# First MLP product of a two-layer trunk: weights stationary replaced by activations stationary, with a TensorE transpose of the squared ReLU

## The chip, the cores and the metric

The kernel runs on one core of one Trainium2 chip. The metric is the device time of one execution in microseconds (us), the median of three runs. Traces come from the hardware profiler: one profiled execution, with the busy time of each engine: PE (TensorE matmul), PEld (TensorE weight load), DVE (VectorE), ACT (ScalarE), POOL (GpSimd) and the SP queue that issues the weight transfers.

## What is computed

A trunk of two layers over 256 tokens of width 2048. Each layer has an attention and SSD part (not touched) and an MLP of width 8192 with squared ReLU:

```python
h = rmsnorm(x, ln2_g)
x = x + jnp.square(jax.nn.relu(h @ w_mlp_in)) @ w_mlp_out
```

All is float32. The norm's scale per token is kept out of `h` and applied (squared) where the second product is added to `x`, which squared ReLU allows.

## The kernel before

Every large product is made of float32r matmuls in three terms: each operand is split into a rounded part `hi` and a remainder `lo`, and the result is hi·hi + hi·lo + lo·hi, summed in PSUM.

The program is a list of **steps**. A step takes half of a weight panel (1024 elements on each of 128 partitions). Panels come by DMA into `raw` (three buffers), 1 MB each. `convert` makes the parts of a half panel: ACT casts `raw` to `hi` (line 121) and DVE subtracts to get `lo` (line 126). The emission loop (line 982) converts four steps ahead (`LA = 4`, five buffers of `hi` and of `lo`), then emits the step's matmuls, then its `post` if it ends an output group, then `tick`, which runs small tasks that are due. ACT, DVE and PE each work their own queue in the order of emission. `stages(f, g)` runs f in the tick right behind the step, and g one step later.

There are two kinds of product:

- `w_units`, **weights stationary**: for each block of 128 weight columns and each k tile of 128 rows, one matmul with 512 moving columns (the activations' whole and low part side by side: `hi` of the weights times both, line 215) and one with 256 (`lo` of the weights times the whole part, line 216; lines 218 and 219 for the last k). A step has 16 matmuls. The result stands transposed, hidden columns on the partitions, and `joined` adds its two halves (lines 425 and 426).
- `x_group`, **activations stationary**: for each k tile and each half of the tokens three matmuls with 512 moving weight columns (lines 291 to 293). A step has 12 matmuls: six for tokens 0 to 127, then six for tokens 128 to 255. The tokens are on the partitions.

Both kinds move 6144 columns per step. The MLP is worked in eight groups of 1024 hidden columns (`GF`). `mlp1(G)` makes `acts[G]`, the squared ReLU, split into hi and lo with the hidden columns on the partitions; `mlp2(G)` uses it as stationary operand. The order is `mlp1(0)`, then for each G `mlp1(G+1)`, `mlp2(G)`. Both have 16 steps a group. Before, `mlp1` is four `w_units` of 256 columns, and `mlp1_post` has for every 128 hidden columns: a copy of half of PSUM by ACT, DVE's sum, DVE's squared ReLU (line 822), and the split by ACT and DVE, on tiles of 128x256. PSUM holds four `acc` buffers, two `sa` and two `sb`.

Of the kernel before, what the change touches and what calls it, by code (L numbers as in the profile page):

```python
# [12 lines left out]
AF = mybir.ActivationFunctionType  # L13
# [18 lines left out]

# Columns of the shape-only constants.
K_ID, K_TRI, K_DIST, K_LNC, K_SEL, K_END = 0, 128, 256, 640, 1024, 1040
# Columns of the packed parameters, channels on the partitions.
V_G1, V_G2, V_GA, V_GS, V_DS, V_CW, V_CB, V_AL, V_DB, V_END = 0, 32, 64, 80, 96, 112, 208, 232, 264, 296
# [17 lines left out]
class Step:  # L54
    """Half a weight panel: its split into two float32r parts, and the products it goes into."""

# [11 lines left out]
def trunk_kernel(ctx: ExitStack, tc, x_in, xT_in, w_in, w_v, w_dt, w_out, w1, w2, final_g, par_in, cst_in, out):  # L68
# [27 lines left out]
    def k1(s="t1", w=T):  # L96
        return k1p.tile([P, w], F32, tag="k1", name=nm(s))
# [19 lines left out]
    def split(*parts):  # L117
        """hi + lo = src * g, each part of twelve significant bits."""
        for hi, lo, src, g in parts:
            if g is None:  # L120
                nc.scalar.copy(hi, src)  # L121
            else:
                nc.scalar.activation(hi, src, AF.Copy, scale=g)
        for hi, lo, src, g in parts:
            if g is None:
                nc.vector.tensor_tensor(lo, src, hi.bitcast(F32), op=ALU.subtract)  # L126
            else:
                nc.vector.scalar_tensor_tensor(lo, src, g, hi.bitcast(F32), op0=ALU.mult, op1=ALU.subtract)  # L128

    mm = nc.tensor.matmul  # L130

# [1 line left out]
    cst = const.tile([P, K_END], F32, name="cst")  # L133
# [51 lines left out]

# [1 line left out]
    tasks = []  # L187
# [14 lines left out]
    def stages(*fs, delay=1):  # L202
        """The first after this step or a later one, each other one a step later."""
        def g():
            for f in fs:
                f()
                yield 1
        spawn(g(), delay)

    steps = []  # L210

# [1 line left out]
    def whole_and_low(ps, wh, wl, r, k):  # L213
# [7 lines left out]
    def w_units(units, hT):  # L221
        """Weights stationary: out[col, token | its low part's products]. Two units at a time share
        the order of k so that the later half of the activations may come late."""
        def unit_steps(u):
            st = {}
            panels = [Panel(u["src"](kh), [P, 8, T]) for kh in range(2)]

            def mk(kq):
                def f(hi, lo):
                    if kq == 0:  # L230
                        st["ps"] = [acc(), acc()]
                    hv = hi.rearrange("p (k c) -> p k c", k=4)
                    lv = lo.rearrange("p (k c) -> p k c", k=4)
                    h = hT()
                    for ti in range(2):
                        ps = st["ps"][ti]
                        cs = slice(ti * P, (ti + 1) * P)
                        for kk in range(4):
                            k = kq * 4 + kk
                            r = h[k // 8][:, k % 8, :]  # L240
                            whole_and_low(ps, hv[:, kk, cs], lv[:, kk, cs], r, k)
                return f

            def post():
                for ti in range(2):
                    u["post"](ti, st["ps"][ti])

            return [Step(panels[kq // 2], kq % 2, mk(kq), post if kq == 3 else None) for kq in range(4)]

        for a in range(0, len(units), 2):  # L250
            ss = [unit_steps(u) for u in units[a:a + 2]]
            if a == 0 and len(ss) == 2:
                steps.extend(ss[0][:2] + ss[1][:2] + ss[0][2:] + ss[1][2:])
            else:
                for s in ss:
                    steps.extend(s)

    def x_group(src, nk, h_of, post, apart=False):
        """Activations stationary: out[token, 512 columns] over nk tiles of k. Apart: all of the first
        128 tokens before the second, and post by their halves."""  # L260
        st = {}
# [38 lines left out]
    def wide(w, l, r0, c0):  # L300
        """The panel of 512 rows and 512 columns from r0, c0."""
        return w[l, r0 // 512, c0 // 512]

    def tall(w, l, r0, c0):
        """The panel of 1024 rows and 256 columns from r0, c0."""
        return w[l, r0 // 1024, c0 // T]

# [1 line left out]
    def new_h():  # L309
# [5 lines left out]
    class Norm:  # L315
        """Sums of squares and split transposes of x, by its chunks of 512 columns."""

# [38 lines left out]
    def channel_rstd(ssq, n):  # L356
        """From squares with the channels on the partitions."""
        ps = sa()
        for t in range(2):
            mm(ps[:, t:t + 1], ssq[:, t * P:(t + 1) * P], ones[:, 0:1], start=True, stop=True)  # L360
        return finish_rstd(ps[:, 0:2], n)

    class FirstNorm:
        """The same from the transposed input, by its chunks of 512 channels."""

# [35 lines left out]

# [1 line left out]
    def layer(l, S, S_next):  # L403
        """S: this layer's state, with hT and norm of its first sub-layer; S_next: the next one's."""
        def rstdB_task():
# [14 lines left out]
        def joined(ps, n=P, scale=None):  # L420
            """The two halves of a weights-stationary product, summed."""
            p2 = p2p.tile([P, T], F32, tag="p2", name=nm("p2"))
            u = k1("u")
            if scale is None:
                nc.scalar.copy(p2[:n], ps[:n, T:2 * T])  # L425
                nc.vector.tensor_tensor(u[:n], ps[:n, 0:T], p2[:n], op=ALU.add)  # L426
            else:
                nc.scalar.mul(p2[:n], ps[:n, T:2 * T], scale)
                nc.vector.scalar_tensor_tensor(u[:n], ps[:n, 0:T], scale, p2[:n], op0=ALU.mult, op1=ALU.add)
            return u  # L430

        # x, B and C: convolution and SiLU, channels on the partitions.
        xs_t, bc_t = {}, {}
# [61 lines left out]

        # dt, the weights' two parts side by side: out[part and head, token | its low part's products].
        dts = {}
# [15 lines left out]
        steps.append(Step(Panel(w_dt[l], [P, 16, 16]), 0, dt_mm, dt_post))  # L513
        # v, tokens on the partitions.
        vt = {}
# [11 lines left out]

# [1 line left out]
        ssd = {}  # L529

        def ssd_prep():
            # dt = softplus(raw + bias), tokens on the partitions.
            ps = sa()
# [34 lines left out]
            yield 2  # L568
            # Running sums of dt * a in each chunk, and the decay to the first chunk's end.
            ps = sa()  # L570
# [48 lines left out]
        def ssd_group(g):  # L619
            """The group's inputs times dt, and its state after the first chunk."""  # L620
            xs, dt, dtd = xs_t["xs"], ssd["dt"], ssd["dtd"]
# [21 lines left out]
        def ssd_pair(j):  # L643
# [3 lines left out]
            for i in range(2):  # L647
                mm(ps[:, i * T:(i + 1) * T], sel[:, 2 * j + i:2 * j + i + 1].to_broadcast([32, P]), cumT,
                   start=True, stop=True)
            # Decays from s to t: where s is later than t, the exponent's bound keeps them finite and  # L650
            # cbs is zero.
            MT = ep.tile([P, 2, T], F32, tag="MT", name=nm("MT"))
# [47 lines left out]

# [1 line left out]
        att = {}  # L702
# [19 lines left out]
        def att_head(j, i):  # L722
            """Softmax of one head's scores; transposed, it is left in att["pt", h]."""
            q, k = att["qk", j, 0], att["qk", j, 1]
# [57 lines left out]

# [1 line left out]
        def out_post(c, which, ps):  # L784
# [28 lines left out]

# [1 line left out]
        acts = {}  # L815

        def mlp1_post(G, f, ps):
            if f == 0:
                acts[G] = new_m()
            u = joined(ps)  # L820
            a = k1("a")
            nc.vector.scalar_tensor_tensor(a, u, 0.0, u, op0=ALU.max, op1=ALU.mult)  # L822
            m = acts[G][:, f, :]
            split((m[:, 0:T], m[:, T:2 * T], a, None))

        def mlp1(G):
            w_units([dict(src=lambda kh, u=u: tall(w1, l, kh * 1024, G * GF + u * T),
                          post=lambda ti, ps, u=u: mlp1_post(G, 2 * u + ti, ps)) for u in range(4)],
                    lambda: S["hT2"])

# [37 lines left out]
    class Final:  # L868
        """The last norm and the output."""

# [46 lines left out]

# [1 line left out]
    panels = []  # L919
# [124 lines left out]
```

## Time and profile before

| | |
|---|---|
| median of 3 runs | 2235.57 us (2235.47 to 2235.91) |
| span of the profiled execution, first to last instruction | 2233.3 us |
| the median less that span | 2.3 us |
| PE busy | 2208.7 us (99%) |
| PEld, DVE, ACT busy | 1850.0, 1460.3, 1058.4 us |
| mean granted TensorE clock | 0.998 of full |

The profiled execution is known by its span; what lies around the span is taken from the timed runs. Matmuls overlap in the records (a matmul's own duration is longer than the distance to the next), so what a matmul costs is read from the distance between starts.

### The profile page before, as it was taken

To read this page: it belongs to the slowest core of one execution; us is meant where nothing else is said; L and a number is where in the kernel's file an instruction comes from. 1 tells how busy PE (TensorE), PEld (TensorE's weight loads), DVE (VectorE), ACT (ScalarE), POOL (GpSimd) and SP (SyncE) were. 2 spreads that over 40 slices of the span, in tenths; PEclk is the share of its full clock that TensorE was granted. 3 is DMA by queue.
4 is the path that set the end of the run, shared out by engine and by line. 5 is a ranking of instruction groups with operands and counts; after the bars stand their busy time and mean duration, and the time that the engine had idled before them with its cause. 6 is when DMAs were issued, how large, how long until landed. Compare 5 with 4: busy or idle time off the path is not lost.

```text
span 2233.3 us, 29120 instructions
## 1 busy us (share of the span) xinstructions
PE 2208.7 (99%) x11444; PEld 1850.0 (83%) x11444; DVE 1460.3 (65%) x1997; ACT 1058.4 (47%) x1539; POOL 150.6 (7%) x201
## 2 busy tenths in 40 slices
PE   8999999999999999999999999999999999999998
PEld 6877778888888888888888777788888888888886
DVE  7757986665665655656666578866656656656565
ACT  6544554543444444434555455555444434444443
POOL 3102310000000000000011032100000000000001
PEclk9999999999999999999999999999999999999999
DMA  8454344555555555555554543455555555555554
GB/s 295 172 188 145 121 151 170 188 188 190 189 189 189 189 188 192 186 196 190 180 188 168 174 150 124 145 186 184 185 190 195 189 189 189 188 191 187 188 193 147
DMA packets 58249, 404.44 MB, mean 181 GB/s; under 512 B 6400, under 2 KB 6784, under 8 KB 10240
## 3 DMA queue, kind: packets, MB, share of 16 engines
q1 hardware_dynamic: 58112, 402.58, 52.1%
q8 instruction: 90, 1.47, 0.3%
q14 instruction: 47, 0.39, 0.0%
HBM read 400.45 MB, written 2.10 MB: 180 GB/s over the span
## 4 chain that ended last, share of the span: by engine, by line
PE 95%; DVE 3%; issue 1%; ACT 0%; DMA 0%; POOL 0%; SPq 0%; ACTq 0%; POOLq 0%; DVEq 0%
PE acc L215 30%; PE acc L216 15%; PE acc L291 14%; PE acc L293 14%; PE acc L292 14%; PE acc L219 2%; PE acc L218 1%; DVE lo L126 1%; PE sb L729 1%; PE sb L728 1%; DMA raw<-in_w_in 0%; PE sb L748 0%; PE sb L765 0%; PE acc L505 0%; DVE h L128 0%
## 5 line engine op out<-in xcount | busy, mean ns | idle before, releaser
L126 DVE TENSOR_TENSOR lo<-raw,hi 128x1024 fp32r<-128x1024 f32 x752 | 921.5, 1235 | 613.4 <-ACT hi L121 613.1
L121 ACT CAST hi<-raw 128x1024 fp32r<-128x1024 f32 x754 | 783.3, 1048 | 718.6 <-PE acc L293 414.2
L215 PE MATMUL acc<-h,hi 128*128 128x512 f32 x3000 | 1077.0, 401 | 8.7 <-DVE h L128 8.7
L216 PE MATMUL acc<-h,lo 128*128 128x256 f32 x3000 | 843.4, 281 | 2.2 <-DVE lo L126 2.2
L215 PEld LDWEIGHTS acc<-h,hi 128*128 128x128 f32 x3000 | 565.3, 188 | 147.1 <-issue 10.2
L216 PEld LDWEIGHTS acc<-h,lo 128*128 128x128 f32 x3000 | 568.3, 189 | 11.4 <-DVE lo L126 2.5
L291 PE MATMUL acc<-hi,m 128*128 128x512 f32 x1280 | 501.0, 391 | 0.0
L293 PE MATMUL acc<-hi,m 128*128 128x512 f32 x1280 | 498.3, 389 | 0.0
L292 PE MATMUL acc<-lo,m 128*128 128x512 f32 x1280 | 498.1, 389 | 0.0
L291 PEld LDWEIGHTS acc<-hi,m 128*128 128x128 f32 x1280 | 240.3, 188 | 51.5 <-issue 3.0
L293 PEld LDWEIGHTS acc<-hi,m 128*128 128x128 f32 x1280 | 240.3, 188 | 50.2
L292 PEld LDWEIGHTS acc<-lo,m 128*128 128x128 f32 x1280 | 240.4, 188 | 49.2
L121 ACT CAST m<-a 128x256 fp32r<-128x256 f32 x128 | 52.1, 407 | 153.6 <-DVE a L822 153.6
L425 ACT COPY p<-acc 128x256 f32<-128x256 f32 x186 | 68.9, 370 | 66.6 <-PE acc L219 61.4
L126 DVE TENSOR_TENSOR m<-a,m 128x256 fp32r<-128x256 f32 x128 | 54.4, 425 | 60.5 <-ACT m L121 60.5
L833 DVE SCALAR_TENSOR_TENSOR x_sb<-acc,r,x_sb 128x512 f32<-128x512 f32 x128 | 89.9, 743 | 4.9 <-PE acc L293 4.9
L426 DVE TENSOR_TENSOR u<-acc,p 128x256 f32<-128x256 f32 x186 | 77.2, 417 | 17.1 <-ACT p L425 17.0
L219 PE MATMUL acc<-h,hi 128*128 128x512 f32 x200 | 80.0, 400 | 0.0
L353 POOL TENSOR_TENSOR rstd<-ms,nhalf 128x2 f32<-128x2 f32 x10 | 8.8, 882 | 873.9 <-DVE ms L351 862.7
L822 DVE SCALAR_TENSOR_TENSOR a<-u 128x256 f32<-128x256 f32 x128 | 54.4, 425 | 4.4
L218 PE MATMUL acc<-h,lo 128*128 128x256 f32 x200 | 56.6, 283 | 0.0
L886 POOL TENSOR_TENSOR x_sb<-x_sb,final_g 128x512 f32<-128x512 f32 x6 | 8.6, 1454 | 687.3 <-DMA final_g<-in_final_norm_g 672.1
(167 smaller groups left out, 1169.7 us busy)
## 6 DMA issues: line engine op xcount, KB each, us to landing
raw<-in_w_mlp_in SPq DMA_DIRECT2D x128, 1024.0 KB, 4.9
raw<-in_w_mlp_out SPq DMA_DIRECT2D x128, 1024.0 KB, 4.9
raw<-in_w_in SPq DMA_DIRECT2D x69, 1024.0 KB, 4.9
raw<-in_w_out SPq DMA_DIRECT2D x32, 1024.0 KB, 4.8
raw<-in_w_v SPq DMA_DIRECT2D x16, 1024.0 KB, 4.9
raw<-in_w_in SPq DMA_DIRECT2D x6, 512.0 KB, 9.0
xT<-in_xT SPq DMA_DIRECT2D x4, 512.0 KB, 8.6
x_sb<-in_x SPq DMA_DIRECT2D x4, 512.0 KB, 6.5
```

Source lines behind the costliest of these rows:

```text
L121: nc.scalar.copy(hi, src)
L126: nc.vector.tensor_tensor(lo, src, hi.bitcast(F32), op=ALU.subtract)
L215: mm(ps, wh, r, start=(k == 0), stop=False)
L216: mm(ps[:, 0:T], wl, r[:, 0:T], start=False, stop=False)
L218: mm(ps[:, 0:T], wl, r[:, 0:T], start=False, stop=False)
L219: mm(ps, wh, r, start=False, stop=True)
L291: mm(ps, ah, hv[:, kk, :], start=(k == 0), stop=False)
L292: mm(ps, ah, lv[:, kk, :], start=False, stop=False)
L293: mm(ps, al, hv[:, kk, :], start=False, stop=(k == nk - 1))
L425: nc.scalar.copy(p2[:n], ps[:n, T:2 * T])
L426: nc.vector.tensor_tensor(u[:n], ps[:n, 0:T], p2[:n], op=ALU.add)
L833: nc.vector.scalar_tensor_tensor(xc, ps[t], S["r2"][:, t:t + 1], xc, op0=ALU.mult, op1=ALU.add)
```

## The change

`mlp1` uses `x_group` in place of `w_units`: two groups of 512 hidden columns for each G, eight steps each, with the activations stationary. The weights come in panels of 512 rows by 512 columns in place of 1024 by 256 (the same bytes, arranged on the host). The squared ReLU is now made on tiles of 128 tokens by 512 hidden columns: ACT writes the ReLU of PSUM (line 824 of the changed kernel), DVE multiplies it by max(PSUM, 0) (line 825). Since `mlp2` wants the hidden columns on the partitions, four TensorE transposes of 128x128 for each half of the tokens (line 832) put them into PSUM, from where ACT and DVE split them. `stages(turn(0), turn(1))` emits the first four transposes right behind the group's last step, the other four one step later. Comments and docstrings go too.

```diff
-        def mlp1_post(G, f, ps):
-            if f == 0:
+        def mlp1_post(G, c, ps):
+
+            if c == 0:
                 acts[G] = new_m()
-            u = joined(ps)
-            a = k1("a")
-            nc.vector.scalar_tensor_tensor(a, u, 0.0, u, op0=ALU.max, op1=ALU.mult)
-            m = acts[G][:, f, :]
-            split((m[:, 0:T], m[:, T:2 * T], a, None))
+            parts = []
+            for t in range(2):
+                r = k2("r")
+                nc.scalar.activation(r, ps[t], AF.Relu)
+                nc.vector.scalar_tensor_tensor(r, ps[t], 0.0, r, op0=ALU.max, op1=ALU.mult)
+                parts.append(r)
+
+            def turn(t):
+                def f():
+                    pt = sa() if t == 0 else sb()
+                    for j in range(4):
+                        nc.tensor.transpose(pt[:, j * P:(j + 1) * P], parts[t][:, j * P:(j + 1) * P], ident)
+                    m = acts[G][:, 4 * c:4 * c + 4, :]
+                    pv = pt.rearrange("p (j n) -> p j n", j=4)
+                    split((m[:, :, t * P:(t + 1) * P], m[:, :, T + t * P:T + (t + 1) * P], pv, None))
+                return f
+
+            stages(turn(0), turn(1))
 
         def mlp1(G):
-            w_units([dict(src=lambda kh, u=u: tall(w1, l, kh * 1024, G * GF + u * T),
-                          post=lambda ti, ps, u=u: mlp1_post(G, 2 * u + ti, ps)) for u in range(4)],
-                    lambda: S["hT2"])
+            for c in range(2):
+                x_group(lambda i, c=c: wide(w1, l, i * 512, G * GF + c * 512), NK,
+                        lambda k: S["hT2"][k // 8][:, k % 8, :], lambda ps, c=c: mlp1_post(G, c, ps))
...
-        "w_dt": w_dt, "w_out": panels(a["w_out"], 512, 512), "w_mlp_in": panels(a["w_mlp_in"], 1024, T),
+        "w_dt": w_dt, "w_out": panels(a["w_out"], 512, 512), "w_mlp_in": panels(a["w_mlp_in"], 512, 512),
```

PE's queue where `mlp1(1)` of the first layer ends and `mlp2(0)` begins, before: `acc_4599` is the last output block of `mlp1`, `h_3562` the second half of the normed activations, `acc_4700` the first output of `mlp2`.

```order
L215 MATMUL acc_4599<-h_3562,hi_4556 128x512
L216 MATMUL acc_4599<-h_3562,lo_4557 128x256
L218 MATMUL acc_4599<-h_3562,lo_4557 128x256
L219 MATMUL acc_4599<-h_3562,hi_4556 128x512
L291 MATMUL acc_4700<-hi_4592,m_4006 128x512
L292 MATMUL acc_4700<-lo_4593,m_4006 128x512
L293 MATMUL acc_4700<-hi_4592,m_4006 128x512
```

The same place of the changed kernel: `acc_4352` is the output for tokens 128 to 255 (that for tokens 0 to 127 is `acc_4351`), `r_4490` the squared ReLU of tokens 0 to 127.

```order
L291 MATMUL acc_4352<-hi_4406,h_3562 128x512
L292 MATMUL acc_4352<-lo_4407,h_3562 128x512
L293 MATMUL acc_4352<-hi_4406,h_3562 128x512
L832 MATMUL sa_4496<-cst,r_4490 128x128 x4
L291 MATMUL acc_4509<-hi_4422,m_4014 128x512
L292 MATMUL acc_4509<-lo_4423,m_4014 128x512
L293 MATMUL acc_4509<-hi_4422,m_4014 128x512
```

Four transposes of `r_4490` now stand between the last matmul of `mlp1` and the first of `mlp2`; those of the other half (`r_4493`) stand one step, 12 matmuls, later.

DVE's queue at that place of the changed kernel: `lo_4475` belongs to the step four ahead of the group's last, and was emitted before that step's matmuls.

```order
L126 TENSOR_TENSOR lo_4457<-raw_4392,hi_4456 128x1024
L126 TENSOR_TENSOR lo_4475<-raw_4392,hi_4474 128x1024
L825 SCALAR_TENSOR_TENSOR r_4490<-acc_4351,r_4490 128x512
L825 SCALAR_TENSOR_TENSOR r_4493<-acc_4352,r_4493 128x512
L126 TENSOR_TENSOR m_4331<-sa_4496,m_4331 128x4x128
L126 TENSOR_TENSOR lo_4504<-raw_4426,hi_4503 128x1024
L126 TENSOR_TENSOR m_4331<-sb_4523,m_4331 128x4x128
```

In place of twelve operations on 128x256 for every 512 hidden columns DVE now has four on 128x512, and PE's next instruction needs the first of them, which stands behind `lo_4475`.

## Rows read from the trace of the kernel before

**Rows 1.** The page: span, busy time by engine, PE's slices and clock.
```profile
span 2233.3 us, 29120 instructions
...
PE 2208.7 (99%) x11444; PEld 1850.0 (83%) x11444; DVE 1460.3 (65%) x1997; ACT 1058.4 (47%) x1539; POOL 150.6 (7%) x201
...
PE   8999999999999999999999999999999999999998
...
PEclk9999999999999999999999999999999999999999
```

**Rows 2.** Busy time by stretch, both MLPs: engines (instructions), clock, DMA share, GB/s.
```profile
408.00:1118.00 710.00, 710.00 (x3606) 603.01 (x3605) 434.36 (x530) 319.52 (x415) 0.69 (x1) 1.00 0.55 189
...
1515.00:2219.00 704.00, 704.00 (x3567) 597.84 (x3566) 427.63 (x516) 312.08 (x400) 9.29 (x7) 1.00 0.54 187
```

**Rows 3.** PE in order of time, mlp1's edges: start, us, instruction.
```profile
542.57 0.39 PE L215 MATMUL acc<-h,hi 128*128 128x512 f32 x1
...
587.46 0.40 PE L219 MATMUL acc<-h,hi 128*128 128x512 f32 x1
587.70 0.40 PE L291 MATMUL acc<-hi,m 128*128 128x512 f32 x1
...
631.23 0.39 PE L215 MATMUL acc<-h,hi 128*128 128x512 f32 x1
```

**Rows 4.** PE in order of time, value product with activations stationary.
```profile
138.86 0.39 PE L291 MATMUL acc<-hi,h 128*128 128x512 f32 x1
...
141.58 0.39 PE L291 MATMUL acc<-hi,h 128*128 128x512 f32 x1
```

**Rows 5.** PE in order of time, four transposes between matmuls.
```profile
157.46 0.40 PE L293 MATMUL acc<-hi,h 128*128 128x512 f32 x1
157.69 0.60 PE L628 MATMUL sa<-cst,xs 128*128 128x128 f32 x4
158.05 0.47 PE L291 MATMUL acc<-hi,h 128*128 128x512 f32 x1
158.37 0.39 PE L292 MATMUL acc<-lo,h 128*128 128x512 f32 x1
```

**Rows 6.** PE in order of time, two batches of four transposes.
```profile
399.04 0.60 PE L335 MATMUL sa<-cst,x_sb 128*128 128x128 f32 x4
399.47 0.60 PE L335 MATMUL sb<-cst,x_sb 128*128 128x128 f32 x4
399.83 0.48 PE L291 MATMUL acc<-hi,m 128*128 128x512 f32 x1
```

**Rows 7.** Instructions of line 628: durations min/median/max.
```profile
L628 PE MATMUL sa<-cst,xs x32: 270/272/275, 157.7 to 1313.2; 128*128 128x128 f32 x32
```

**Rows 8.** All engines in order of time, one step of mlp2.
```profile
520.81 0.39 PE L291 MATMUL acc<-hi,m 128*128 128x512 f32 x1
...
521.01 1.06 ACT L121 CAST hi<-raw 128x1024 fp32r<-128x1024 f32 x1 [1.67 <-PE acc L293]
...
522.09 1.23 DVE L126 TENSOR_TENSOR lo<-raw,hi 128x1024 fp32r<-128x1024 f32 x1 [0.17 <-ACT hi L121]
...
523.53 0.39 PE L291 MATMUL acc<-hi,m 128*128 128x512 f32 x1
```

**Rows 9.** DVE in order of time, two operations on PSUM behind a remainder.
```profile
530.25 1.22 DVE L126 TENSOR_TENSOR lo<-raw,hi 128x1024 fp32r<-128x1024 f32 x1 [1.50 <-ACT hi L121]
531.39 1.40 DVE L833 SCALAR_TENSOR_TENSOR x_sb<-acc,r,x_sb 128x512 f32<-128x512 f32 x2
```

**Rows 10.** Last matmul for tokens 0 to 127, and ACT's first reader.
```profile
156.07 0.39 PE L293 MATMUL acc<-hi,h 128*128 128x512 f32 x1
...
156.51 0.69 ACT L521 ACTIVATE v<-acc,rstd 128x512 f32<-128x512 f32 x1 [1.87 <-PE acc L293]
```

**Rows 11.** Groups by line: busy, mean ns of one, idle before.
```profile
L833 DVE SCALAR_TENSOR_TENSOR x_sb<-acc,r,x_sb 128x512 f32<-128x512 f32 x128 | 89.9, 743 | 4.9 <-PE acc L293 4.9
...
L640 ACT COPY S<-sa 128x512 f32<-128x512 f32 x4 | 2.3, 586 | 13.1 <-PE sa L638 13.1
```

**Rows 12.** DVE and PE in order of time, PE released by DVE.
```profile
250.12 1.21 DVE L665 TENSOR_TENSOR MT<-MT,cbs 128x512 f32<-128x512 f32 x1
...
251.39 0.44 PE L674 MATMUL sa<-MT,X 128*64 128x128 f32 x4 [0.98 <-DVE MT L665]
251.66 0.39 PE L676 MATMUL sa<-MT,X 128*64 128x128 f32 x4
```

**Rows 13.** The page's DMA issues: issues, KB each, us to landing.
```profile
raw<-in_w_mlp_in SPq DMA_DIRECT2D x128, 1024.0 KB, 4.9
raw<-in_w_mlp_out SPq DMA_DIRECT2D x128, 1024.0 KB, 4.9
```

## The prediction

> **What bounds the kernel now.** The page comes first: PE is busy for 99% of the span, with nine tenths or more in nearly every slice and the clock at its upper level of 2.4 GHz throughout, while DVE has 65% and ACT 47% [rows 1]. A busy PE in a record is not yet a PE that is never held up, so the busy time by stretch comes next: in both MLPs PE is busy for 710.00 of 710.00 us and 704.00 of 704.00 us, at a granted clock of 1.00 [rows 2]. In these 1414 us, where all of the change lies, nothing but the spacing of PE's instructions makes time. DVE and ACT can give back as much as they like there; only what PE does or waits for counts. So the last view is PE in order of time, read by starts: a matmul's recorded 0.39 us overlaps the next one.
>
> **The first product's step, before and after (a gain).** One `mlp1(G)` runs from 542.57 to 587.70, 45.13 us for 16 steps (2.821 us a step); the `mlp2` behind it has 16 steps too and runs to 631.23, 43.53 us (2.721 us a step) [rows 3]. Both move 6144 columns a step; the one does it with 16 matmuls, the other with 12. The changed `mlp1` has the form of `mlp2`, with the normed activations `h` stationary instead of `m`. That form is in the trace as well: in the value product twelve matmuls with `h` stationary take 141.58 - 138.86 = 2.72 us, 0.2267 us each [rows 4], as with `m`. So the changed `mlp1` takes 43.53 us in place of 45.13, and 1.60 us go in each of 16 groups (two layers by eight): **-25.6 us**.
>
> The Trainium skill, TensorE: Matmul & The Clock Gate, section Back-to-back issue gap, speaks against this gain: it gives a warm gap of N / 2.4 + 2.5 ns. By it the 512 and 256 columns would take 215.8 and 109.2 ns, a step 2.600 us before and 2.590 us after, and the gain would be an estimated 2.6 us in all, the sum then about 23 us worse. The trace does not agree: 226.7 ns for 512 columns, and 2.821 us for the eight pairs [rows 3, 4]. I take the rows.
>
> **The transposes (a loss).** Each group of 512 columns adds eight, in two batches of four; there are 32 such groups, so 64 batches and 256 transposes. The trace has the same operation, four 128x128 float32 transposes between matmuls with 512 columns: they start at 157.69, the next matmul at 158.05, and the one behind it only at 158.37 [rows 5]. From 157.69 to 158.37 is 0.68 us, of which one matmul is 0.227; the batch costs 0.453 us. 64 x 0.453 = **+29.0 us**. Bounds: where two batches stand together the second takes 399.83 - 399.47 = 0.36 us [rows 6], and the whole recorded time of a batch is 0.60 us [rows 5]. I take 0.453, since there, as in the change, a batch stands alone.
>
> **The wait ahead of the first batch (a loss).** The order shows that `turn(0)` is emitted right behind the last matmul of a group. It needs the squared ReLU of tokens 0 to 127, which ACT and DVE must first make. PE works in order, so whatever is late there stops the matmuls behind it. I take 0 as the start of the group's last step and follow the three queues.
>
> PE: matmuls every 0.2267 us; the sixth, last for tokens 0 to 127, starts at 1.13, and the step's twelve are through at 2.72. ACT: the cast for the step four ahead starts 521.01 - 520.81 = 0.20 into a step and lasts 1.06 [rows 8], so ACT is free at 1.26. The first reader of a finished half group starts 156.51 - 156.07 = 0.44 after the last matmul's start [rows 10]: the ReLU starts at 1.57 and is done at 2.16, by the 586 ns of ACT's copy of the same shape out of PSUM [rows 11]. DVE: the remainder for the step four ahead starts 522.09 - 520.81 = 1.28 into the step [rows 8], and in DVE's queue it stands ahead of the squaring. In `mlp2` two operations on 128x512 from PSUM, of the same kind as the squaring, start 531.39 - 530.25 = 1.14 after the remainder's start [rows 9] and last 743 ns each [rows 11]. So the squaring ends at 1.28 + 1.14 + 0.74 = 3.16. PE goes on 0.06 after DVE's end, as where 250.12 + 1.21 = 251.33 released it at 251.39 [rows 12]: at 3.22, against 2.72. PE loses 0.50 us in each of 32 groups: **+16.0 us**.
>
> Bounds: if the remainder were not in the way, the squaring could start at 2.16, end at 2.90, and PE would go on at 2.96: 0.24 us. If the transposes had to wait for the second half's squaring as well, 1.40 - 0.74 = 0.66 us would be added [rows 9]: 1.16 us. I take 0.50, since each of its pieces is from a step of the same form, in which DVE and ACT follow the same period.
>
> The second batch doesn't wait: the second squaring ends at about 3.8, and PE comes to that batch at 3.22 + 0.45 + 2.72 = 6.4.
>
> **What costs nothing.** DVE had twelve operations on 128x256 for 512 columns and now has four on 128x512; ACT has four in place of eight. That is less work on engines that PE doesn't wait for [rows 2], worth 0; without that cover nothing would be lost, as it is a saving. Behind the wait ACT's split of the first batch delays the cast for the step five ahead: the split can start at about 3.22 + 0.45 + 0.2 = 3.9 and ends at 4.5, the cast at 5.5, DVE's remainder at about 6.8. PE needs it five steps later, at about 3.7 + 4 x 2.72 + 0.45 = 15, so some 8 us cover it; if the cover were gone, PE would lose that lateness in each group. `acts[G]` is wanted an `mlp2` of 43.53 us later, except for G = 0, where an `mlp1` lies between. The weights come in the same 128 pieces of 1 MB, landing in 4.9 us [rows 13], at the same two steps a panel. The first `mlp1` of a layer reads k tiles 0 to 7 in its first four steps before and after, so late norm transposes are no nearer.
>
> **The sum.** -25.6 + 29.0 + 16.0 = +19.4 us. The profiled span of 2233.3 becomes 2252.7 us. The median of the timed runs stands 2.3 us above that span; with the same added, **2255 us**, 0.87% slower. What a measurement of this kernel can tell from no change is about 0.2%, 4.5 us.
>
> **The rivals.** *Faster: the transposes and the wait cost PE less than the shorter steps give.* This needs 64 batches and 32 waits below 25.6 - 4.5 = 21.1 us: without any wait a batch below 0.33 us. At 0.20 us a batch and no wait, it would be 2235.6 + 12.8 - 25.6 = 2223 us. Against it: no batch in the trace is below 0.36 [rows 6], and even with a free DVE the chain of ReLU and squaring ends 0.24 late. Chance 0.04.
>
> *Little wait, and so nearly no change.* If DVE came to the squaring early, the wait would be 0.24: 7.7 + 29.0 - 25.6 = +11.1, 2247 us; with none at all +3.4, 2239 us. For it: DVE is idle for a third of the time. Against it: the remainder's place in the step is periodic [rows 8, 9]. Chance 0.08, 0.04 of it within 0.2%.
>
> *A longer wait.* If PE is held until both halves are squared, 1.16 us: 37.1 + 29.0 - 25.6 = +40.5, 2276 us. Against it: the order shows that only `r` of the first half is read there. Chance 0.08.
>
> *Transposes one after another.* If each cost its recorded 272 ns [rows 7], 256 would be 69.6 us, the sum +60.0, 2296 us. The distance of starts speaks against it: four in 0.453 [rows 5]. Chance 0.02. The Trainium skill, TensorE: Matmul & The Clock Gate, section Part 4: PE-mode transpose, gives about 275 ns in one kernel's context, which would come to that; the trace has it as a duration and not as a distance.
>
> *The change doesn't do what it says: steps of 12 matmuls are no shorter in `mlp1`.* Then nothing pays for the rest: +45.0, 2281 us. Rows 4 speak against it by the same operand and form; chance 0.02. The Trainium skill's formula named above would have nearly this result.
>
> **How the numbers follow.** The forecast has 0.76. Its own range takes waits of 0.40 to 0.70 and batches of 0.42 to 0.50: 12.8 + 26.9 - 25.6 = +14.1 to 22.4 + 32.0 - 25.6 = +28.8, 2250 to 2264 us. The ends of the bounds together are 7.7 + 23.0 - 25.6 = +5.1 and 37.1 + 38.4 - 25.6 = +49.9, 2241 and 2285; to leave out no more than 2 in 10 I widen the forecast's range to 2246 to 2268, which takes in the larger of the two cases of little wait. Faster 0.04, same 0.04, slower 0.92: the forecast and the other cases all end slower.
>
> **What would show it.** In the profile after: steps of `mlp1` of 2.72 us away from the group ends; four transposes with about 0.45 us between the matmuls around them, 64 times; 32 waits of PE at line 832 for DVE at line 825, of about 0.5 us, and none ahead of the second batch; in each group 43.53 + 2 x 0.50 + 4 x 0.453 = 46.3 us for `mlp1`. It is wrong if those waits are missing or twice as long, if the transposes keep the matmuls behind them slow for longer, or if the granted clock of the MLP falls below 1.00 after the waits.

## The result and the profile after

The changed kernel takes 2258.24 us (median of 4 runs, 2258.16 to 2258.56), against 2235.52 us of the kernel before on the same chip: a ratio of 1.0102, 95% interval 1.0087 to 1.0116. The forecast was 2255 us, in a range of 2246 to 2268. The profiled span grew from 2233.3 to 2256.4 us, by 23.1 us; the sum had +19.4.

The page after, as in [rows 1]:

```profile
span 2256.4 us, 27014 instructions
...
PE 2218.2 (98%) x10676; PEld 1821.1 (81%) x10676; DVE 1400.7 (62%) x1741; ACT 1047.0 (46%) x1411; POOL 150.5 (7%) x201
...
PEclk9999999999999999999999999999999999999999
```

PE has 768 instructions fewer and is busy longer; DVE lost 60 us of work and ACT 11, and neither shows in the time. The stretch that answers to [rows 3], by PE in order of time and by busy time in two windows, one `mlp1` and the `mlp2` behind it (columns as in [rows 2]):

```profile
545.35 0.39 PE L291 MATMUL acc<-hi,h 128*128 128x512 f32 x1
...
591.32 0.47 PE L291 MATMUL acc<-hi,m 128*128 128x512 f32 x1
...
635.45 0.39 PE L291 MATMUL acc<-hi,h 128*128 128x512 f32 x1
```

```profile
545.35:591.32 45.97, 45.22 (x205) 36.98 (x204) 24.09 (x24) 20.20 (x22) 0.00 (x0) 1.00 0.55 185
591.32:635.45 44.13, 44.13 (x200) 36.54 (x198) 25.77 (x26) 17.82 (x18) 0.00 (x0) 1.00 0.55 189
```

A group of `mlp1` and `mlp2` took 45.13 + 43.53 = 88.66 us [rows 3] and now takes 90.10, which in 16 groups is 23.0 us: all of the difference. The twelve groups of the trace that stand in this order agree within 0.03 us in each kernel. The clock in both windows is 1.00. For the first time in the MLP PE is not busy throughout: 0.75 us of the first window are missing, in two pieces. The list of what PE waited for names them, with the sum in us, the number of waits and the longest:

```profile
PE sa L832 <- DVE r L825: 12.0, 32, 0.4
```

Here is one of the 32, at a group's end, on PE, ACT and DVE:

```profile
589.72 0.39 PE L291 MATMUL acc<-hi,h 128*128 128x512 f32 x1
589.94 0.39 PE L292 MATMUL acc<-lo,h 128*128 128x512 f32 x1
590.17 0.39 PE L293 MATMUL acc<-hi,h 128*128 128x512 f32 x1
590.94 0.63 PE L832 MATMUL sa<-cst,r 128*128 128x128 f32 x4 [0.38 <-DVE r L825]
591.32 0.47 PE L291 MATMUL acc<-hi,m 128*128 128x512 f32 x1
591.63 0.39 PE L292 MATMUL acc<-lo,m 128*128 128x512 f32 x1
```

```profile
589.24 0.60 ACT L824 ACTIVATE r<-acc 128x512 f32<-128x512 f32 x1 [0.30 <-PE acc L293]
590.60 0.60 ACT L824 ACTIVATE r<-acc 128x512 f32<-128x512 f32 x1 [0.76 <-PE acc L293]
```

```profile
588.96 1.23 DVE L126 TENSOR_TENSOR lo<-raw,hi 128x1024 fp32r<-128x1024 f32 x1 [1.50 <-ACT hi L121]
590.11 0.68 DVE L825 SCALAR_TENSOR_TENSOR r<-acc,r 128x512 f32<-128x512 f32 x1
591.23 0.69 DVE L825 SCALAR_TENSOR_TENSOR r<-acc,r 128x512 f32<-128x512 f32 x1 [0.43 <-ACT r L824]
```

The step began at 587.68, where its first matmul followed those of the step before. The figures worked out in the prediction stand in brackets: the ReLU starts 1.56 into the step (1.57), DVE's remainder 1.28 (1.28), the squaring 2.43 (2.42), and it ends at 590.79, 3.11 in (3.16). PE would have gone on at 590.40 and starts the transposes at 590.94: 0.54 us. The bracket shows only 0.38, since the last matmul's record reaches 0.16 past the slot that it takes; the distance of starts is the lost time. The second batch, one step later, has no wait:

```profile
593.94 0.40 PE L293 MATMUL acc<-hi,m 128*128 128x512 f32 x1
594.18 0.60 PE L832 MATMUL sb<-cst,r 128*128 128x128 f32 x4
594.53 0.48 PE L291 MATMUL acc<-hi,m 128*128 128x512 f32 x1
594.85 0.39 PE L292 MATMUL acc<-lo,m 128*128 128x512 f32 x1
595.08 0.40 PE L293 MATMUL acc<-hi,m 128*128 128x512 f32 x1
595.32 0.39 PE L291 MATMUL acc<-hi,m 128*128 128x512 f32 x1
595.55 0.40 PE L292 MATMUL acc<-lo,m 128*128 128x512 f32 x1
```

From 593.94 to 594.85 is 0.91 us with two matmuls of 0.227 in it: 0.457 us for the batch, against 0.453 of [rows 5]. The matmuls behind it, from 594.85 to 595.55, start 0.233 apart and not 0.2267.

### The profile page after: what moved, and what is told of

The parts are those of the page before. It is cut to its first block, busy times and chain, and to the rows that moved or that the text cites. A ratio compares the mean times of both kernels' runs of the same rounds, so it can differ in the third digit from the quotient of the medians.

```text
span 2256.4 us, 27014 instructions
## 1 busy us (share of the span) xinstructions
PE 2218.2 (98%) x10676; PEld 1821.1 (81%) x10676; DVE 1400.7 (62%) x1741; ACT 1047.0 (46%) x1411; POOL 150.5 (7%) x201
## 4 chain that ended last, share of the span: by engine, by line
PE 91%; DVE 5%; ACT 2%; issue 1%; DMA 0%; POOL 0%; SPq 0%; ACTq 0%; POOLq 0%; DVEq 0%
PE acc L291 23%; PE acc L293 23%; PE acc L292 23%; PE acc L215 10%; PE acc L216 5%; DVE lo L126 2%; ACT hi L121 2%; PE sa L832 1%; DVE r L825 1%; PE acc L219 1%; PE sb L832 1%; PE sb L729 1%; PE sb L728 1%; DMA raw<-in_w_in 0%; PE sb L748 0%
## 5 line engine op out<-in xcount | busy, mean ns | idle before, releaser
L291 PE MATMUL acc<-hi,h 128*128 128x512 f32 x1152 | 454.9, 395 | 0.0
L293 PE MATMUL acc<-hi,h 128*128 128x512 f32 x1152 | 449.3, 390 | 0.0
L292 PE MATMUL acc<-lo,h 128*128 128x512 f32 x1152 | 448.7, 390 | 0.0
L215 PE MATMUL acc<-h,hi 128*128 128x512 f32 x1080 | 393.7, 405 | 7.9 <-DVE h L128 7.9
L216 PE MATMUL acc<-h,lo 128*128 128x256 f32 x1080 | 304.3, 282 | 3.1 <-DVE lo L126 3.1
L215 PEld LDWEIGHTS acc<-h,hi 128*128 128x128 f32 x1080 | 203.9, 189 | 63.2 <-issue 10.2
L293 PEld LDWEIGHTS acc<-hi,h 128*128 128x128 f32 x1152 | 216.3, 188 | 45.6
L291 PEld LDWEIGHTS acc<-hi,h 128*128 128x128 f32 x1152 | 216.4, 188 | 44.8 <-issue 0.8
L292 PEld LDWEIGHTS acc<-lo,h 128*128 128x128 f32 x1152 | 216.5, 188 | 43.8 <-issue 0.5
L216 PEld LDWEIGHTS acc<-h,lo 128*128 128x128 f32 x1080 | 205.2, 190 | 6.4 <-DVE lo L126 3.4
L824 ACT ACTIVATE r<-acc 128x512 f32<-128x512 f32 x64 | 38.3, 598 | 34.2 <-PE acc L293 34.2
```

Of the source, the lines that this page charges most:

```text
L215: mm(ps, wh, r, start=(k == 0), stop=False)
L216: mm(ps[:, 0:T], wl, r[:, 0:T], start=False, stop=False)
L291: mm(ps, ah, hv[:, kk, :], start=(k == 0), stop=False)
L292: mm(ps, ah, lv[:, kk, :], start=False, stop=False)
L293: mm(ps, al, hv[:, kk, :], start=False, stop=(k == nk - 1))
L824: nc.scalar.activation(r, ps[t], AF.Relu)
```

## The experiments

The theory is the prediction's sum: the shorter steps give time back, the transposes and the waits ahead of half of them take it. The first five runs take the sum apart; the last four ask where the shorter steps come from. Each ratio is to the kernel before on the same chip; runs on different chips are compared by their distance from it.

**Transposes one step later.** Edit:

```diff
-            stages(turn(0), turn(1))
+            stages(turn(0), turn(1), delay=2)
```

> The changed kernel with turn(0) and turn(1) each emitted one step later, nothing else. Theory (the 32 waits ahead of the first batch are lost time of their own, 0.53 us each): the waits of PE at the transposes go, 32 x 0.53 = 17 us come back, about 2241 us, and the 64 batches still cost 0.45 us each. Rival (PE would wait for something of the squared ReLU wherever the transposes stand, or the lost time shows again elsewhere): about 2258 us.

Measured: 2240.56 us, ratio to before 1.0021 (1.0012 to 1.0031). All waits at line 832 are gone from the list, and the four transposes follow the matmul in its normal slot:

```profile
590.04 0.39 PE L293 MATMUL acc<-hi,m 128*128 128x512 f32 x1
590.27 0.60 PE L832 MATMUL sa<-cst,r 128*128 128x128 f32 x4
590.62 0.48 PE L291 MATMUL acc<-hi,m 128*128 128x512 f32 x1
```

The excess over before falls from 22.7 to 4.6 us. The waits are lost time of their own and come back whole; they were a matter of where the transposes stand. What stays, 4.6 us, is 1.2 more than the prediction's sum with no wait (+3.4).

**No transposes.** The first `turn` and the second split `parts[t]` as it stands, so the second product works on other numbers of the same shape:

```diff
-                    pt = sa() if t == 0 else sb()
-                    for j in range(4):
-                        nc.tensor.transpose(pt[:, j * P:(j + 1) * P], parts[t][:, j * P:(j + 1) * P], ident)
                     m = acts[G][:, 4 * c:4 * c + 4, :]
-                    pv = pt.rearrange("p (j n) -> p j n", j=4)
+                    pv = parts[t].rearrange("p (j n) -> p j n", j=4)
```

> The changed kernel without the transposes: the squared ReLU is split as it stands, tokens on the partitions, so the second product multiplies other numbers, by the same number of instructions of the same shapes. Theory (the shorter steps give 25.6 us, and transposes with their waits cost all that is lost): the 32 x 1.01 + 32 x 0.46 = 47 us seen at the transposes go, 2211 us, that is 24 to 26 us below before. Rival (steps of 12 matmuls are no gain in the first product, or ACT's and DVE's new work costs something): 2225 us or more.

Measured: 2209.66 us, ratio 0.9883 (0.9867 to 0.9900), 26.3 us below before; the step's shape was worked out as -25.6. The form with activations stationary is faster, and ACT's and DVE's changed work costs nothing. The run with the transposes one step later, on the same chip, is 30.9 us slower than this one: that is what 64 batches cost without a wait, 0.48 us each.

**The kernel before with the transposes added**, of a constant, without a reader:

```diff
             split((m[:, 0:T], m[:, T:2 * T], a, None))
+            if f % 4 == 3:
+                def turn(t):
+                    def f():
+                        pt = sa() if t == 0 else sb()
+                        for j in range(4):
+                            nc.tensor.transpose(pt[:, j * P:(j + 1) * P], cst[:, K_DIST:K_DIST + P], ident)
+                    return f
+
+                stages(turn(0), turn(1))
```

> The kernel before with the change's transposes added in the same number and at the same distance (four behind every 512 hidden columns, four a step later), but of a constant that is long there, and with no reader. Theory (a batch costs PE 0.45 us beside the matmuls in front and behind, whatever it waits for): 64 x 0.453 = +29 us, 2264 us, with no wait at them. Rival (transposes fit in the room that the short matmuls with 256 columns leave, and cost less): under 2255 us.

Measured: 2261.85 us, ratio 1.0117 (1.0102 to 1.0132), +25.9 us: nearer to +29 than to the rival's bound, 3 us short of it. At the batches the price is as worked out:

```profile
592.16 0.39 PE L219 MATMUL acc<-h,hi 128*128 128x512 f32 x1
592.39 0.60 PE L830 MATMUL sa<-cst 128*128 128x128 f32 x4
592.74 0.47 PE L291 MATMUL acc<-hi,m 128*128 128x512 f32 x1
593.06 0.39 PE L292 MATMUL acc<-lo,m 128*128 128x512 f32 x1
```

0.90 less 0.453 is 0.45. What is missing from the 29 us lies in the weights-stationary steps behind a batch. In the middle of a group, two whole steps there start 2.77 and 2.79 us before the next, where undisturbed ones in the same group take 2.83:

```profile
575.53 0.39 PE L215 MATMUL acc<-h,hi 128*128 128x512 f32 x1
...
578.30 0.39 PE L215 MATMUL acc<-h,hi 128*128 128x512 f32 x1
...
581.09 0.39 PE L215 MATMUL acc<-h,hi 128*128 128x512 f32 x1
...
583.90 0.40 PE L215 MATMUL acc<-h,hi 128*128 128x512 f32 x1
...
586.73 0.40 PE L215 MATMUL acc<-h,hi 128*128 128x512 f32 x1
```

Why pairs of a long and a short matmul run closer for a while behind a batch stays open.

**The squaring ahead of the remainder.** In the last step of a first-product group the conversion of the step four ahead is emitted behind the squared ReLU:

```diff
+                steps[-1].late = True
...
         for i, s in enumerate(steps):
+            late = getattr(s, "late", False)
+            if late:
+                s.mm(s.hi, s.lo)
+                s.post()
             if i + LA < len(steps):
...
-            s.mm(s.hi, s.lo)
-            if s.post is not None:
-                s.post()
+            if not late:
+                s.mm(s.hi, s.lo)
+                if s.post is not None:
+                    s.post()
```

> The changed kernel, but in the last step of each first-product group the conversion of the step four ahead is emitted behind the squared ReLU and not in front of it; the transposes stay where they are. Theory (of the wait of 0.53 us DVE's remainder, which stands ahead of the squaring, makes 0.3, the chain of ReLU and squaring the rest): waits of about 0.23 us, 10 us back, about 2248 us. Rival (the chain alone, or the transposes' own start, makes the wait): 2256 us or more; rival (the late conversion holds up PE four steps later): above 2258 us.

Measured: 2250.66 us, ratio 1.0067 (1.0052 to 1.0082), 14.7 above before in place of 22.7, and 2.7 above what the theory had.

```profile
590.16 0.39 PE L293 MATMUL acc<-hi,h 128*128 128x512 f32 x1
590.70 0.63 PE L832 MATMUL sa<-cst,r 128*128 128x128 f32 x4
```

```profile
589.86 0.69 DVE L825 SCALAR_TENSOR_TENSOR r<-acc,r 128x512 f32<-128x512 f32 x1 [2.40 <-ACT r L824]
```

DVE now idles 2.40 us and takes the squaring as soon as ACT's ReLU is done; it ends at 590.55, the transposes start 0.15 later, and the wait is 590.70 - 590.39 = 0.31 us. So DVE's remainder made 0.23 of the 0.54, and the chain of ReLU, squaring and release 0.31. Both rivals fall: the remainder does have a part, and the time stays below 2258 us. The chain was taken for 0.23: between the squaring's end and the transposes lie 0.15 us here and in the changed kernel, not the 0.06 of [rows 12].

**Sixteen transposes in one place.** The `turn`s of both halves of a group of 1024 are held back and run together, one step behind its end:

```diff
+        held = []
...
-            stages(turn(0), turn(1))
+            held.extend([turn(0), turn(1)])
+            if c == 1:
+                def all_turns(fs=list(held)):
+                    for f in fs:
+                        f()
+                held.clear()
+                stages(all_turns, delay=2)
```

> The changed kernel with all 16 transposes of a group of 1024 hidden columns in one place, one step behind the group's end. Theory (no wait there, and batches that follow one another cost 0.36 us, as where two stand together in the trace of before, so 0.45 + 3 x 0.36 = 1.53 us in each of 16 groups, 24.6 us): 2258.2 - 46.9 + 24.6 = 2236 us, level with before. Rival (each batch costs 0.45 wherever it stands): 2240 us. Rival (four splits in a row hold up ACT's and DVE's conversions until PE waits for weights): above 2245 us.

Measured: 2238.4 us, ratio 1.0011 (1.0002 to 1.0020), 2.4 above before.

```profile
588.86 0.40 PE L293 MATMUL acc<-hi,m 128*128 128x512 f32 x1
589.10 0.60 PE L833 MATMUL sa<-cst,r 128*128 128x128 f32 x4
589.53 0.60 PE L833 MATMUL sb<-cst,r 128*128 128x128 f32 x4
589.97 0.60 PE L833 MATMUL sa<-cst,r 128*128 128x128 f32 x4
590.40 0.60 PE L833 MATMUL sb<-cst,r 128*128 128x128 f32 x4
590.76 0.48 PE L291 MATMUL acc<-hi,m 128*128 128x512 f32 x1
591.07 0.40 PE L292 MATMUL acc<-lo,m 128*128 128x512 f32 x1
```

Batches that follow one another start 0.43 apart, and all sixteen cost 591.07 - 588.86 - 0.453 = 1.76 us, 0.44 a batch. The 0.36 of [rows 6] was misread: it left out that the matmul behind the batch is followed late (0.31 in place of 0.227). So the estimate of 2236 is too low and the first rival nearer. This best form of the change is still not faster than before: the transposes eat all of the 26 us.

**Long and short matmuls apart.** In the kernel before, within each block of 128 hidden columns of a step of the first product, the four matmuls of 512 columns come ahead of the four of 256:

```diff
-    def w_units(units, hT):
+    def w_units(units, hT, apart=False):
...
+                        if apart:
+                            for kk in range(4):
+                                k = kq * 4 + kk
+                                mm(ps, hv[:, kk, cs], h[k // 8][:, k % 8, :], start=(k == 0), stop=False)
+                            for kk in range(4):
+                                k = kq * 4 + kk
+                                mm(ps[:, 0:T], lv[:, kk, cs], h[k // 8][:, k % 8, 0:T], start=False,
+                                   stop=(k == NK - 1))
+                            continue
                         for kk in range(4):
...
-                    lambda: S["hT2"])
+                    lambda: S["hT2"], apart=True)
```

> The kernel before, but within each 128 hidden columns of a step of the first MLP product the four matmuls with 512 moving columns come first and the four with 256 behind them; same matmuls, same loads. It asks why a step of 16 matmuls takes 0.10 us more than one of 12 with as many columns. Theory A (a fixed cost for every matmul, about 0.0135 us beyond the columns at 2.4 GHz, whatever stands next to it): 2235.5 us, no change. Theory B (a 256-column matmul is too short to cover the next weight load, recorded at 0.188 us, and only the long ones beside it make up for that): each short one stretches towards 0.188 us from 0.115, up to 8 x 0.07 = 0.6 us a step, up to 150 us in 256 steps, so above 2300 us.

Measured: 2232.12 us, ratio 0.9983 (0.9974 to 0.9992): 3.9 us faster. Theory B falls. Theory A, by which what stands next to a matmul does not matter, misses as well: the order is worth 3.9 us in 2048 pairs of a long and a short one, 1.9 ns a pair. The cost of a matmul as such is tested by the next run.

```profile
543.90 0.64 PE L244 MATMUL acc<-h,lo 128*128 128x256 f32 x4
544.37 1.09 PE L241 MATMUL acc<-h,hi 128*128 128x512 f32 x4
545.30 0.63 PE L244 MATMUL acc<-h,lo 128*128 128x256 f32 x4
545.77 1.09 PE L241 MATMUL acc<-h,hi 128*128 128x512 f32 x4
```

Four short ones take 0.47 us, 0.1175 each, though each has its own weight load recorded at 0.189; four long ones take 0.93, 0.2325 each.

**The changed kernel with its matmuls cut in halves.** For 14 of the 16 k tiles each matmul of 512 columns of the first product becomes two of 256:

```diff
-    def x_group(src, nk, h_of, post, apart=False):
+    def x_group(src, nk, h_of, post, apart=False, halves=False):
...
+                if halves and 0 < k < nk - 1:
+                    for w, m in ((ah, hv), (ah, lv), (al, hv)):
+                        for cs in (slice(0, 256), slice(256, 512)):
+                            mm(ps[:, cs], w, m[:, kk, cs], start=False, stop=False)
+                    continue
...
-                        lambda k: S["hT2"][k // 8][:, k % 8, :], lambda ps, c=c: mlp1_post(G, c, ps))
+                        lambda k: S["hT2"][k // 8][:, k % 8, :], lambda ps, c=c: mlp1_post(G, c, ps), halves=True)
```

> The changed kernel with each matmul of the first product, but for the first and last of its 16 k tiles, cut into two of 256 moving columns: 84 matmuls more in each of 64 groups of 128 tokens by 512 columns... that is 2688 more in all with their weight loads, the same columns. Theory (a matmul costs its columns and about 0.0125 us, so that two of 256 take 0.235 to 0.240 us in place of 0.2267): +22 to +36 us, 2280 to 2294 us. Rival (a 256-column matmul alone can't cover its own weight load of 0.188 us): two take 0.376 us, +400 us. Rival (the number of matmuls does not matter, only which operand stands still): 2258 us.

The 2688 is right; it is 84 more in each of 32 groups of 512 columns, 42 for each half of the tokens, not 84 in each of 64. Measured: 2288.93 us, ratio 1.0237 (1.0222 to 1.0253), 30.7 us above the changed kernel, with the operands and the columns unchanged. Not all of the cost shows in the 30.7, since the waits ahead of the transposes are shorter in this run, 5.7 us in place of 12.0:

```profile
592.32 0.64 PE L294 MATMUL acc<-hi,h 128*128 128x256 f32 x4
...
594.48 0.64 PE L294 MATMUL acc<-hi,h 128*128 128x256 f32 x4
```

```profile
PE sa L837 <- DVE r L830: 5.7, 32, 0.2
```

With these 6.3 us the 2688 matmuls cost 37 us, 13.8 ns each. The distances of starts say the same: between the two rows start 18 matmuls, 2.16 / 18 = 0.120 us each, so that two of 256 take 0.240 us in place of 0.2267. It is the number of matmuls, each with its weight load, that counts; both rivals fall.

**That order in every weights-stationary product.** In the kernel before, for all of `w_units`:

```diff
                         for kk in range(4):
                             k = kq * 4 + kk
-                            r = h[k // 8][:, k % 8, :]
-                            whole_and_low(ps, hv[:, kk, cs], lv[:, kk, cs], r, k)
+                            mm(ps, hv[:, kk, cs], h[k // 8][:, k % 8, :], start=(k == 0), stop=False)
+                        for kk in range(4):
+                            k = kq * 4 + kk
+                            mm(ps[:, 0:T], lv[:, kk, cs], h[k // 8][:, k % 8, 0:T], start=False,
+                               stop=(k == NK - 1))
```

> The kernel before with the order of e6_long_then_short in every weights-stationary product, not in the MLP alone: 3200 pairs in place of 2048. Theory (each pair gains the 1.9 ns that e6_long_then_short gained): 2235.9 - 6.0 = 2230 us. Rival (that gain belongs to the MLP, where nothing else runs on PE): 2232 us.

Measured: 2229.59 us, ratio 0.9975 (0.9965 to 0.9985), 6.0 us faster, as worked out for 3200 pairs; the rival had 2232 us and falls.

**Eight and eight.** All long matmuls of a step, both blocks of 128 columns, then all short ones:

```diff
                         for kk in range(4):
                             k = kq * 4 + kk
-                            r = h[k // 8][:, k % 8, :]
-                            whole_and_low(ps, hv[:, kk, cs], lv[:, kk, cs], r, k)
+                            mm(ps, hv[:, kk, cs], h[k // 8][:, k % 8, :], start=(k == 0), stop=False)
+                    for ti in range(2):
+                        ps = st["ps"][ti]
+                        cs = slice(ti * P, (ti + 1) * P)
+                        for kk in range(4):
+                            k = kq * 4 + kk
+                            mm(ps[:, 0:T], lv[:, kk, cs], h[k // 8][:, k % 8, 0:T], start=False,
+                               stop=(k == NK - 1))
```

> As e8_all_long_then_short, but all eight 512-column matmuls of a step first and then all eight of 256. Theory (what is lost is lost where long and short alternate): below e8_all_long_then_short by 1 us or more, 2229 us or less. Rival (a run of four is enough): the same as that.

Measured: 2226.91 us, ratio 0.9960 (0.9948 to 0.9973): 8.7 us below before, 31 below the changed kernel, and 2.7 below four and four, so that a run of four is not enough. It is faster than both kernels, without a transpose.

```profile
560.54 1.12 PE L246 MATMUL acc<-h,lo 128*128 128x256 f32 x8
561.49 2.00 PE L240 MATMUL acc<-h,hi 128*128 128x512 f32 x8
563.33 1.11 PE L246 MATMUL acc<-h,lo 128*128 128x256 f32 x8
564.28 2.00 PE L240 MATMUL acc<-h,hi 128*128 128x512 f32 x8
```

A step is 564.28 - 561.49 = 2.79 us, against 2.82 before and 2.72 with twelve long matmuls. Its eight long matmuls take 563.33 - 561.49 = 1.84 us, 0.230 each.

## Why the prediction was right

**The bound.** PE sets the time in the MLP, and ACT and DVE only where PE waits for them at line 832. The run without transposes shows it, where ACT and DVE work as in the change and the time falls to what PE's steps alone give; and so does the change itself, where 60 us less work on DVE gave nothing back.

**The shorter steps (-25.6).** Measured -26.3 in the run without transposes. The form with `h` stationary could be priced because the value product had it [rows 4]. The cause was not in the prediction: a step of 16 matmuls has four more than one of 12, and by the run with halves each costs some 14 ns beside its columns. That price was measured with activations stationary; carried over to the steps with weights stationary, four times 13.8 ns is 0.055 us of the 0.100 per step. The order of long and short, tried by itself, brings a step from 2.82 to 2.79 us, another 0.03. The remaining 0.02 us a step stay open; sorted long matmuls still follow one another 0.230 us apart there and not 0.2267.

**The transposes (+29.0).** Without waits they cost 30.9 us. At the batch it is 0.457 us, as worked out; left out was what follows. At the first batch of a group, wait and transposes together take 591.63 - 590.17 - 0.453 = 1.007 us, at the second 0.457; twice both is 2.93 us for 1024 hidden columns. The windows show 90.10 - 88.66 + 1.60 = 3.04. The other 0.11 us lie in the step behind each batch, where matmuls start up to 0.233 us apart instead of 0.2267: some 2 us in 16 groups. The prediction had named matmuls that stay slow behind the transposes as a sign of being wrong; it came, at a size that the range covers. The lower bound of 0.36 us a batch was misread from [rows 6], where the second batch costs 0.44 with what follows it, so the case against a faster kernel was stronger than stated. And of the four batches in the 46.3 us given for `mlp1` only three lie in its window, which is 45.97.

**The wait (+16.0).** 0.54 us instead of 0.50, 17 us in 32. The three queues start as worked out, within 0.01 us. Two sizes were off and cancel in part, which is luck: the squaring is 55 ns shorter than DVE's other operation of its shape (0.688 against 0.743), and the release of the transposes takes 0.15 us instead of 0.06. Why the release takes longer here stays open. The run with the transposes one step later shows that the wait is lost time, and the run with the squaring first shows that DVE's remainder makes less than half of it; the prediction's lower bound, without the remainder, had 0.24, and 0.31 was measured. The second squaring ends at 591.92, 4.24 into the step and not 3.8, as its ReLU must wait for the group's last matmul; it costs nothing, since PE comes to the second batch at 6.50 (6.4). But a wait for both halves would have cost an estimated 4.24 + 0.15 - 2.72 = 1.67 us and not the 1.16 of the rival.

**The sum.** +19.4 was forecast, and the span has +23.1: 1.8 us more at the waits and batches themselves (32 x 1.464 = 46.8 against 45.0), some 2 us in the steps behind them.

**The rivals.** None came. That of no wait at all is the run with the transposes one step later, 4.6 us above before: its price was near (+3.4), its condition was not met. Transposes one after another at their recorded 272 ns would have cost 70 us; without a wait 26 us were seen in the kernel before, 29 with all sixteen together and 31 with each batch a step later. That steps of twelve are no gain is refuted by the run without transposes. The Trainium skill's formula for the gap (TensorE: Matmul & The Clock Gate, section Back-to-back issue gap) puts 2.5 ns on each matmul beside its columns; by it the halves would have cost an estimated 2688 x 2.5 ns = 7 us. No run here agrees: 37 us were measured, 13.8 ns each, in matmuls that each have a weight load of their own. The section itself gives the formula for a matmul by itself and says that in a stream with weight loads both set the spacing.

## What to carry to other kernels

Where PE is the bound, a change of which operand stands still is priced by the number of matmuls, the columns and what must be turned: here four matmuls fewer in each of 256 steps went with 26 us less, and 256 transposes without a wait took back 29 to 31. A PE instruction that needs a result of ACT and DVE belongs a step behind the matmuls that feed it; emitted right behind them, it holds up an engine that had no idle time, here for 0.54 us each time. And look at the order within a step before its form: here long and short matmuls sorted into runs gave 8.7 us with no other change.

## What was not expected of the hardware

A matmul of 256 columns with its own weight load, recorded at 0.189 us, follows the one before in 0.1175 us in a run of its kind: the recorded time of a load is not a floor there. Long and short matmuls alternating cost more than sorted: 0.353 us a pair in `mlp1` before (2.82 us a step), 0.350 in runs of four, 0.349 in runs of eight (2.79 us a step). Four float32 transposes make a batch of 0.44 to 0.46 us, alone or in a row, but leave a trace behind: the step with activations stationary just after one is slower by some 0.03 us, while steps with weights stationary are faster (2.77 us against 2.83).
